# A third pair of k-tiles in the last sweep of w_down, three residues of that sweep by accumulating DMA

## The chip, the cores and the metric

One core of one Trainium2 chip runs the kernel. The metric is device time in microseconds (us) of one execution. TensorE is called PE here, VectorE DVE, ScalarE ACT, GpSimd POOL and SyncE SP, as in the profile; a name with a trailing "q" is that engine's sequencer.

## The reference

The kernel computes one layer of a residual block for 256 tokens of width 2048, in float32. The part in front (differential attention beside a convolution, and their output projection) is not touched. The change is in the last matrix product of the second half:

```python
hn = rms_norm(h, norm2_g[l])
a = jnp.einsum('bsd,df->bsf', hn, w_gate[l].astype(hn.dtype))      # 2048 -> 5632
bu = jnp.einsum('bsd,df->bsf', hn, w_up[l].astype(hn.dtype))       # 2048 -> 5632
h = h + jnp.einsum('bsf,fd->bsd', jax.nn.silu(a) * bu, w_down[l].astype(hn.dtype))
```

## The kernel before, in words

**Precision.** PE reads float32r. Every operand is split into a rounded part `hi` and a residue `lo`, and each product is three matmuls: hi by hi, lo by hi, hi by lo. For a tile of weights, `raw` is loaded by SP (L320), ACT rounds it into `whi` (L325) and DVE subtracts to get `wlo` (L334). There is a second way to the residue, used where `by_dma` is set: ACT writes the negative of the rounded weights into `wlo` (L328), and POOL issues a DMA (L329) that adds `raw` into it, from SBUF to SBUF; DVE then has nothing to do for that tile.

**The hidden width in groups.** The 5632 hidden columns are 11 blocks of 512, that is 4 k-tiles of 128 each, taken in groups of 4, 4 and 3 blocks (`FGROUPS`). After the gate and up products of a group's blocks follows a pass of `w_down` over the k-tiles of that group (`down_pass`). A pass has two sweeps: the first makes the output columns 0 to 1023, the second 1024 to 2047. In a sweep the left 512 columns are called g and the right 512 u. The last group (g = 2) has 12 k-tiles.

**Pairs and twos.** In a sweep some k-tiles are taken as pairs: tile p with tile p + 4, against both column halves at once. The 2 x 2 blocks of a pair are multiplied with seven products in place of eight (`PRODUCTS`, L1046 to L1048: 7 x 3 = 21 matmuls), for which sums of the four weight blocks are formed: on DVE L1019, L1020 and L1021 write the sums `wt`; ACT rounds the blocks (L1022) and the sums (L1025); DVE makes the residues `wlb` (L1028) and `wlt` (L1029). A pair's first four products use the sums, so its third matmul is the first that reads `wlt`. The other k-tiles go as "twos": two k-tiles against one column half, 12 matmuls (L1067, L1068, and L1073 for the last four, which read `wlo`). The sums of the activations that a pair needs are made once for a group (`make_down_forms`, L903 to L944), from `raw_act`, to which the transposed activations are copied (`transposed`); `NDS` gives the number of pairs for which these forms are made.

**The order of units.** `DORDERS` writes out the order in a sweep: s is a pair, g and u are twos. I number the units of the last group's sweeps: A0 to A9 for the first ("gguusggsuu", pairs A4 and A7), B0 to B9 for the second ("gggsgsuuuu", pairs B3 and B5). The program runs one unit after another (`run_chunks`). Before the matmuls of unit t are issued, units up to t + 2 are split (residues on DVE; for a pair also ACT's L1025) and units up to t + 3 are loaded and rounded (for a pair also DVE's sums and ACT's L1022; for a two by DMA also ACT's L328 and POOL's L329), where a pair is among t to t + 3; elsewhere it is t + 2 for both. Each engine works its instructions in that order, so the order of these steps is the order on DVE, ACT and POOL. Buffers: five `raw`, three `whi`, three `wlo`, two `wb` (a pair's weights), one `wt`. A load is issued when the unit that had its buffer has been split, or, for a unit by DMA, when that unit's turn has come.

**The end of a sweep.** Once the last unit that isn't a u is done, ACT copies one bank (L1156) and DVE adds the seven products up (L1158 to L1163, `bank_sums`); after the last u the other half follows. For the first sweep of the last group POOL then adds the four results into `hd` in DRAM (L1210 twice, L1238 twice, behind DVE's L1226), SP fetches the other half of `hd` (`hend`, L1200), and some units later POOL copies the finished half of `hd` to the output (L1245, twice), which waits for these four. For the second sweep DVE adds into `hend` (L1212, L1217, L1278, L1231), and that goes to the output. All DMAs issued by POOL are on one queue (q0), all by SP on another (q1).

Of the kernel before, what the change touches and what calls it, by code (L numbers as in the profile page):

```python
# [84 lines left out]
ORDER = "sggsggsuusuu"  # L85
# [1 line left out]


HD = N // P
NDS = (4, 4, 2)  # L90
DORDERS = {4: (ORDER, ORDER), 3: ("gguusggsuu", "gggsgsuuuu")}
HD_LAG = 3
DOWN_BY_DMA = {4: (dict(g=(0, 1), u=(1,)),) * 2, 3: (dict(g=(), u=()),) * 2}

Q1, Q6, Q7, Q5, Q2, Q4, Q3, QX = range(8)

# [31 lines left out]
def tile_block(  # L128
# [6 lines left out]
    act, dve, pool, pe, sp = nc.scalar, nc.vector, nc.gpsimd, nc.tensor, nc.sync  # L135
# [96 lines left out]
    def lhs_two(pfx, k):  # L232
        return tuple(lhs.tile([P, 2, S], F32R, tag=f"l{x}", name=f"{pfx}{x}{k}") for x in ("hi", "lo"))
# [12 lines left out]
    def start(gen):  # L246
        running.append(gen)
# [7 lines left out]
    def lag(n):  # L255
        for _ in range(n):
            yield
# [593 lines left out]
    def up_done(j, ps):  # L851
        fp = ffn["pool"]
        aa = []
        for m in range(NM):
            a = fp.tile([P, N], F32, tag=f"sum{2 + m}", name="a")
            dve.scalar_tensor_tensor(a, ps[m], rstd2[m], sil[m], ALU.mult, ALU.mult)
            aa.append(a)
        yield from lag(4)
        yield from transposed(j, aa)

    def transposed(j, aa):
        last = j + 1 in FIRSTS and NDS[group_of(j)[0]] < HD
        b = j - group_of(j)[1]
        for t in range(N // P // 2):

            pool_, tag = (acc_ps, "acc") if last else (aux_ps, "aux")
            pt = pool_.tile([P, 2, S], F32, tag=tag, name="ps_a")
            for i in range(2):
                for m in range(NM):
                    c = (2 * t + i) * P  # L870
                    pe.transpose(pt[:, i, m * P : (m + 1) * P], aa[m][:, c : c + P], ident)  # L871
            g = group_of(j)[0]
            nd = NDS[g]
            if b < 2 and 2 * t < nd:
                if not b and not t:
                    raw_act[g] = ffn["pool"].tile([P, 2, nd, S], F32, tag="draw", name="raw_act")
                act.copy(raw_act[g][:, b, 2 * t : 2 * t + 2, :], pt)
                yield from lag(3 if last else 6)
                if b and 2 * t + 2 == nd:
                    start(make_down_forms(g))  # L880
                continue
            hi, lo = lhs_two("a", j * (N // P) + 2 * t)
            act.copy(hi, pt)
            yield from lag(1 if last else 2)
            dve.tensor_tensor(lo, pt, hi.bitcast(F32), ALU.subtract)
            for i in range(2):
                actT[j * (N // P) + 2 * t + i] = (hi[:, i, :], lo[:, i, :])
            yield from lag(1 if last else 3 if closing(j) else 4)

    def closing(j):  # L890
        return j + 1 in FIRSTS and NDS[group_of(j)[0]] == HD

    def group_of(j):

        j0 = 0
        for g, nb in enumerate(FGROUPS):
            if j < j0 + nb:
                return g, j0
            j0 += nb

    raw_act = {}
    down_forms = {}

    def make_down_forms(g):

        nd = NDS[g]
        gap = lambda: lag(5 if FGROUPS[g] == 4 else 2)
# [195 lines left out]
    def fast_block(order, pairs, twos, sources, operands, half, whole, by_dma=dict(g=(), u=())):  # L1103

        units, sums = [], {}
        left = dict(s=list(pairs), g=list(twos), u=list(twos))
        for kind in order:
            what = left[kind].pop(0)
            c = dict(kind=kind, sums=sums, done=None, first={}, last={}, rows=what["rows"], **operands)
            if kind == "s":  # L1110
                c.update(p=what["p"], fetch=load_pair, by_dma=False, round=round_pair, split=split_pair, multiply=multiply_pair,
                         uses=[q for q, _, _ in PRODUCTS])
                c["from"] = sources
            else:
                w, col = sources[kind]
                c.update(ks=what["ks"], w=w, nk=2, width=N, cols=[(col, N)], by_dma=what["k"] in by_dma[kind],
                         load=load_chunk, round=round_chunk, split=split_chunk, multiply=multiply_two,
                         uses=(Q3, QX) if kind == "u" else (Q2, Q4))
            units.append(c)
        assert not any(left.values())  # L1120
        for q in range(8):
            users = [c for c in units if q in c["uses"]]
            users[0]["first"][q] = users[-1]["last"][q] = True
        [c for c in units if c["kind"] != "u"][-1]["done"] = half
        units[-1].update(done=whole, prompt=True)
        chunks.extend(units)
# [8 lines left out]

    def down_pass(g, j0, nb):
        k0 = j0 * HD
        nd = NDS[g]
        ks = [k for k in range(nb * HD) if k >= 2 * HD or k % HD >= nd]
        twos = [dict(ks=(k0 + a, k0 + b), rows=slice(k0 + a, k0 + b + 1, b - a), k=i)  # L1140
                for i, (a, b) in enumerate(zip(ks[::2], ks[1::2]))]
        for i, order in enumerate(DORDERS[nb]):
            n = 2 * i
            end = {}
            fast_block(order, [dict(p=p, rows=slice(k0 + p, k0 + p + HD + 1, HD)) for p in range(nd)], twos,
                       dict(g=(w_down, n * N), u=(w_down, (n + 1) * N)),
                       dict(pairs=lambda: down_forms.get(g), plain=actT.get),
                       lambda sums, n=n, end=end: down_half(g, n, sums, end),
                       lambda sums, n=n, end=end: down_whole(g, n, sums, end), DOWN_BY_DMA[nb][i])

# [23 lines left out]
    def block_done(j, q):  # L1174
        while "u" not in halfway:
            yield
        u = halfway.pop("u")
        for m, i in enumerate((Q3, QX)):
            dve.tensor_tensor(u[m], q[i], u[m], ALU.add)
        while "g" not in halfway:  # L1180
            yield
        g = halfway.pop("g")
        for m in range(NM):
            dve.tensor_tensor(u[m], u[m], g[m], ALU.mult)
        yield from lag(6 if closing(j) else 4)
        yield from transposed(j, u)
# [15 lines left out]
    def down_half(g, n, q, end):  # L1202
        gs, us = yield from bank_sums(q)
        if not at_end(g, n):
            end.update(us=us)
            yield from lag(HD_LAG)
        for m in range(NM):
            cs = slice(n * N, (n + 1) * N)
            if not at_end(g, n):
                pool.dma_start(out=hd[m][:, cs], in_=gs[m], accum_op=ALU.add)  # L1210
            else:
                dve.tensor_tensor(hend[m][:, :N], hend[m][:, :N], gs[m], ALU.add)  # L1212
                pool.dma_start(out=out[m * P : (m + 1) * P, cs], in_=hend[m][:, :N])
        yield
        if at_end(g, n):
            for m in range(NM):
                dve.tensor_tensor(hend[m][:, N:], hend[m][:, N:], us[m], ALU.add)  # L1217
        end.update(us=us)

    def down_whole(g, n, q, end):  # L1220
        while "us" not in end:
            yield
        us = end["us"]
        for m, i in enumerate((Q3, QX)):
            if not at_end(g, n):
                dve.tensor_tensor(us[m], q[i], us[m], ALU.add)  # L1226
                continue
            w = N // 2
            for a in range(0, N, w):
                hs = hend[m][:, N + a : N + a + w]  # L1230
                dve.tensor_tensor(hs, hs, q["ends"][a // w] if m else q[i][:, a : a + w], ALU.add)  # L1231
                (act if m and a else sp).dma_start(
                    out=out[m * P : (m + 1) * P, (n + 1) * N + a : (n + 1) * N + a + w], in_=hs)
        if not at_end(g, n):
            if FGROUPS[g] > 3:
                yield from lag(HD_LAG)
            for m in range(NM):
                pool.dma_start(out=hd[m][:, (n + 1) * N : (n + 2) * N], in_=us[m], accum_op=ALU.add)  # L1238
        if g == len(FGROUPS) - 1 and not at_end(g, n):
            fetch_end()  # L1240

            yield from lag(6)
            for m in range(NM):
                cs = slice(n * N, (n + 2) * N)
                pool.dma_start(out=out[m * P : (m + 1) * P, cs], in_=hd[m][:, cs])  # L1245
# [87 lines left out]
```

## Time and profile before

| | |
|---|---|
| median of three runs | 1036.0 us (1035.3 to 1036.17) |
| the profiled execution | 1035.99 us |
| its span, first to last instruction | 1034.2 us |
| mean granted PE clock | 1.000 |
| busy: PE, DVE, ACT, POOL | 1028.1, 927.3, 638.3, 108.7 us |
| PE, 998.4 to 1019.5 us of the span | 20.87 of 21.10 us busy |
| DVE, the same stretch | 20.10 us busy |
| ACT, the same stretch | 11.28 us busy |

The last pass of `w_down` begins at about 966 us; its first sweep ends at 998.4, its second at about 1030. Rows of a timeline give the start in us of the span, the duration in us, the engine, the line, the operation with output and input, the shapes and how many instructions were merged; brackets give the idle time just ahead and what ended it. A row with "x3" covers three instructions back to back. Durations on PE overlap, as matmuls are pipelined; the distance between starts is the pace.

### The profile page before, as it was taken

The numbers are of one execution on the slowest core, as the hardware profiler recorded it, in microseconds if no ns is written. First come the engines' busy times: TensorE is split into PE (matmuls) and PEld (weight loads), VectorE is DVE, ScalarE is ACT, GpSimd is POOL, SyncE is SP. The second block draws the span as 40 slices with busy tenths as digits, with TensorE's granted clock in tenths as the row PEclk, the third lists the DMA queues.
The fourth block names the chain that finished last, engine by engine and source line by source line (L and its number), as shares of the span: only waits on it lengthen the run. The fifth ranks groups of instructions, "written<-read, shape, count | busy, mean of one in ns | idle before, by whom it ended". The sixth has DMA issues, their size and how long they took to land.

```text
span 1034.2 us, 13010 instructions
## 1 busy us (share of the span) xinstructions
PE 1028.1 (99%) x4645; PEld 848.9 (82%) x4645; DVE 927.3 (90%) x1126; ACT 638.3 (62%) x780; POOL 108.7 (11%) x147
## 2 busy tenths in 40 slices
PE   9999999999999999999999999999999999999998
PEld 7888888888888888888888888888888888888886
DVE  7899999989766699999999898989999989989887
ACT  7554656655666575677666556667657556667452
POOL 0130112111000100100102111001001111000010
PEclk9999999999999999999999999999999999999999
DMA  9657654553546677987989899879798979797773
GB/s 340 225 182 276 215 175 145 183 183 135 183 171 223 189 258 226 286 256 211 260 260 257 265 255 271 267 225 261 230 270 248 280 214 298 231 262 230 218 219 106
DMA packets 115664, 237.59 MB, mean 230 GB/s; under 512 B 7696, under 2 KB 8848, under 8 KB 115344
## 3 DMA queue, kind: packets, MB, share of 16 engines
q1 hardware_dynamic: 104720, 203.58, 59.0%
q0 software_dynamic: 10592, 33.04, 16.5%
q8 instruction: 36, 0.59, 0.2%
q14 instruction: 28, 0.23, 0.1%
q10 hardware_dynamic: 288, 0.16, 0.1%
HBM read 204.24 MB, written 9.44 MB: 207 GB/s over the span
## 4 chain that ended last, share of the span: by engine, by line
PE 96%; DVE 2%; DMA 1%; issue 1%; ACT 0%; SPq 0%; DVEq 0%
PE acc L364 11%; PE acc L365 11%; PE acc L370 11%; PE q L1067 11%; PE q L1068 11%; PE q L1073 11%; PE q L1048 9%; PE q L1046 9%; PE q L1047 9%; PE ps_a L871 1%; DVE wlo L334 1%; DMA raw<-in_w_in_dram 1%; PE ps_s L692 1%; PE ps_o L762 1%; DVE wlt L1029 0%
## 5 line engine op out<-in xcount | busy, mean ns | idle before, releaser
L325 ACT CAST whi<-raw 128x1024 fp32r<-128x1024 f32 (+1 forms) x257 | 266.4, 1047 | 149.7 <-PE acc L365 87.5
L334 DVE TENSOR_TENSOR wlo<-raw,whi 128x1024 fp32r<-128x1024 f32 (+1 forms) x211 | 254.6, 1217 | 37.9 <-ACT whi L325 37.8
L1025 ACT CAST wh<-wt 128x2048 fp32r<-128x2048 f32 x60 | 114.9, 1915 | 108.8 <-DVE wt L1021 108.7
L1029 DVE TENSOR_TENSOR wlt<-wt,wh 128x2048 fp32r<-128x2048 f32 x60 | 137.4, 2290 | 19.5 <-ACT wh L1025 19.4
L364 PE MATMUL acc<-whi,xhi 128*128 128x512 f32 x320 | 127.2, 398 | 0.7 <-ACT whi L325 0.6
L1067 PE MATMUL q<-whi,chi 128*128 128x512 f32 x320 | 125.2, 391 | 0.0
L365 PE MATMUL acc<-whi,xlo 128*128 128x512 f32 x320 | 125.1, 391 | 0.0
L1068 PE MATMUL q<-whi,clo 128*128 128x512 f32 x320 | 124.6, 389 | 0.0
L1046 PE MATMUL q<-wh,fhi 128*128 128x512 f32 x280 | 109.9, 392 | 0.0
L1047 PE MATMUL q<-wh,flo 128*128 128x512 f32 x280 | 108.9, 389 | 0.0
L1028 DVE TENSOR_TENSOR wlb<-wb,wh 128x1536 fp32r<-128x1536 f32 x60 | 105.1, 1751 | 1.1 <-ACT wh L1022 1.1
L553 DVE SCALAR_TENSOR_TENSOR y<-upad,cw,y 128x256 f32<-128x256 f32 x240 | 102.2, 485 | 2.2 <-ACT y L546 2.2
L329 POOL DMA_DIRECT2D wlo<-raw x46 | 39.8, 865 | 508.0 <-ACT wlo L328 283.4
L1022 ACT CAST wh<-wb 128x1536 fp32r<-128x1536 f32 x60 | 88.3, 1472 | 0.0
L370 PE MATMUL acc<-wlo,xhi 128*128 128x512 f32 x320 | 87.1, 393 | 0.0
L1073 PE MATMUL q<-wlo,chi 128*128 128x512 f32 x320 | 85.6, 389 | 0.0
L1067 PE MATMUL q<-whi,ahi 128*128 128x512 f32 x190 | 74.1, 390 | 0.0
L1068 PE MATMUL q<-whi,alo 128*128 128x512 f32 x190 | 74.0, 389 | 0.0
L1019 DVE TENSOR_TENSOR wt<-wb 128x1024 f32<-128x1024 f32 x60 | 73.1, 1218 | 0.0
L364 PEld LDWEIGHTS acc<-whi,xhi 128*128 128x128 f32 x320 | 60.3, 189 | 14.5 <-ACT whi L325 2.0
L365 PEld LDWEIGHTS acc<-whi,xlo 128*128 128x128 f32 x320 | 60.3, 188 | 12.3
L1073 PEld LDWEIGHTS q<-wlo,chi 128*128 128x128 f32 x320 | 60.1, 188 | 12.6
(253 smaller groups left out, 1836.3 us busy)
## 6 DMA issues: line engine op xcount, KB each, us to landing
raw<-in_w_in_dram SPq DMA_DIRECT2D x79, 512.0 KB, 4.7
raw<-in_w_gate_dram SPq DMA_DIRECT2D x48, 512.0 KB, 5.3
raw<-in_w_up_dram SPq DMA_DIRECT2D x48, 512.0 KB, 5.3
raw<-in_w_down_dram SPq DMA_DIRECT2D x48, 512.0 KB, 6.4
wlo<-raw POOLq DMA_DIRECT2D x46, 512.0 KB, 7.1
wb<-in_w_up_dram SPq DMA_DIRECT2D x40, 512.0 KB, 4.5
wb<-in_w_gate_dram SPq DMA_DIRECT2D x40, 512.0 KB, 5.8
wb<-in_w_down_dram SPq DMA_DIRECT2D x40, 512.0 KB, 6.0
```

The costliest lines, as they stand in the source:

```text
L325: act.copy(c["hi"], c["raw"])
L334: dve.tensor_tensor(c["lo"], c["raw"], c["hi"].bitcast(F32), ALU.subtract)
L364: pe.matmul(ps[m], xhi[:, ms], hi[:, j, :], start=c["first"] and j == 0, stop=False)
L365: pe.matmul(ps[m], xlo[:, ms], hi[:, j, :], start=False, stop=False)
L370: pe.matmul(ps[m], xhi[:, ms], lo[:, j, :], start=False, stop=c["last"] and j == nk - 1)
L1025: act.copy(c["hi"][:, :SUMMED], c["t"])
L1029: dve.tensor_tensor(lot, c["t"], c["hi"][:, :SUMMED].bitcast(F32), ALU.subtract)
L1046: pe.matmul(ps, hi, c["hi"][:, w], start=bool(first), stop=False)
L1047: pe.matmul(ps, lo, c["hi"][:, w], start=False, stop=False)
L1067: pe.matmul(ps, xs[i][0][:, ms], hi[:, i, :], start=i == 0 and bool(c["first"].get(qs[m])), stop=False)
L1068: pe.matmul(ps, xs[i][1][:, ms], hi[:, i, :], start=False, stop=False)
L1073: pe.matmul(sum_bank(c, qs[m]), xs[i][0][:, ms], lo[:, i, :], start=False, stop=i == 1 and bool(c["last"].get(qs[m])))
```

## The change

The second sweep of the last group takes three pairs (k-tiles 0 to 2 of the group with 4 to 6) and six twos, in the order "gsgsgsuuu": pairs B1, B3 and B5, and units B0 to B8. The first sweep keeps two pairs. The forms of that group are made for three pairs, and the k-tiles 2 and 6, which are twos in the first sweep and a pair in the second, are kept in both shapes. In the second sweep the residues of the first two g twos (B0, B2) and of the first u two (B6) go by accumulating DMA; before, none in these two sweeps did.

```diff
-NDS = (4, 4, 2)
-DORDERS = {4: (ORDER, ORDER), 3: ("gguusggsuu", "gggsgsuuuu")}
+NDS = (4, 4, 3)
+PASS_PAIRS = ((4, 4), (4, 4), (2, 3))
+DORDERS = {4: (ORDER, ORDER), 3: ("gguusggsuu", "gsgsgsuuu")}
 HD_LAG = 3
-DOWN_BY_DMA = {4: (dict(g=(0, 1), u=(1,)),) * 2, 3: (dict(g=(), u=()),) * 2}
+DOWN_BY_DMA = {4: (dict(g=(0, 1), u=(1,)),) * 2, 3: (dict(g=(), u=()), dict(g=(0, 1), u=(0,)))}
...
                     raw_act[g] = ffn["pool"].tile([P, 2, nd, S], F32, tag="draw", name="raw_act")
-                act.copy(raw_act[g][:, b, 2 * t : 2 * t + 2, :], pt)
-                yield from lag(3 if last else 6)
-                if b and 2 * t + 2 == nd:
+                end = min(2 * t + 2, nd)
+                act.copy(raw_act[g][:, b, 2 * t : end, :], pt[:, : end - 2 * t])
+                if 2 * t + 2 <= PASS_PAIRS[g][0]:
+                    yield from lag(3 if last else 6)
+                if b and end == nd:
                     start(make_down_forms(g))
-                continue
+                if 2 * t + 2 <= PASS_PAIRS[g][0]:
+                    continue
...
     def down_pass(g, j0, nb):
         k0 = j0 * HD
-        nd = NDS[g]
-        ks = [k for k in range(nb * HD) if k >= 2 * HD or k % HD >= nd]
-        twos = [dict(ks=(k0 + a, k0 + b), rows=slice(k0 + a, k0 + b + 1, b - a), k=i)
-                for i, (a, b) in enumerate(zip(ks[::2], ks[1::2]))]
         for i, order in enumerate(DORDERS[nb]):
+            nd = PASS_PAIRS[g][i]
+            ks = [k for k in range(nb * HD) if k >= 2 * HD or k % HD >= nd]
+            twos = [dict(ks=(k0 + a, k0 + b), rows=slice(k0 + a, k0 + b + 1, b - a), k=i)
+                    for i, (a, b) in enumerate(zip(ks[::2], ks[1::2]))]
             n = 2 * i
```

## The prediction

> **What bounds the kernel now.** I read the page first, for the bound and the time outside the span; then the timelines of PE, DVE, ACT, POOL and SP over the last 80 us, because the edit acts there; then the DMA view of the same stretch.
>
> ```profile
> span 1034.2 us, 13010 instructions
> PE 1028.1 (99%) x4645; PEld 848.9 (82%) x4645; DVE 927.3 (90%) x1126; ACT 638.3 (62%) x780; POOL 108.7 (11%) x147
> PE 96%; DVE 2%; DMA 1%; issue 1%; ACT 0%; SPq 0%; DVEq 0%
> ```
>
> PE is the bound: it is busy for 99% of the span and is 96% of the chain that ended last. The profiled execution took 1035.99 us: 1034.2 of span and 1.8 around it. It sits on the median of the runs (1036.0), so a change of the span is added to 1036.0 directly. A difference under about 0.2% (2.07 us) can't be told from no change.
>
> The units of the sweep that changes, in the naming above, stand on PE like this. The rows of L1067 and L1046 are first matmuls: of B0, B1, B3, B4, B5, B6 and the last unit, B9. The two of L1048 are the third matmuls of the pairs B3 and B5:
>
> ```profile
> 998.36 0.39 PE L1067 MATMUL q<-whi,ahi 128*128 128x512 f32 x1
> 1001.08 0.39 PE L1067 MATMUL q<-whi,ahi 128*128 128x512 f32 x1
> 1006.52 0.39 PE L1046 MATMUL q<-wh,dhs 128*128 128x512 f32 x1
> 1007.03 0.50 PE L1048 MATMUL q<-wlt,dhs 128*128 128x512 f32 x1
> 1011.47 0.39 PE L1067 MATMUL q<-whi,ahi 128*128 128x512 f32 x1
> 1014.19 0.39 PE L1046 MATMUL q<-wh,dhs 128*128 128x512 f32 x1
> 1015.03 0.50 PE L1048 MATMUL q<-wlt,dhs 128*128 128x512 f32 x1 [0.23 <-DVE wlt L1029]
> 1019.47 0.39 PE L1067 MATMUL q<-whi,ahi 128*128 128x512 f32 x1
> 1027.63 0.39 PE L1067 MATMUL q<-whi,ahi 128*128 128x512 f32 x1
> ```
>
> B0, twelve matmuls, takes 1001.08 - 998.36 = 2.72 us, so a matmul costs 0.2267 us and a pair of 21 should take 4.76. The two pairs took 1011.47 - 1006.52 = 4.95 and 1019.47 - 1014.19 = 5.28: stalls of 0.19 and 0.52, 0.71 together, both at the third matmul, the first that reads the residue `wlt`. So here PE is the bound with DVE right behind it.
>
> **What goes from PE.** The second sweep had 2 pairs and 8 twos, 2 x 21 + 8 x 12 = 138 matmuls; now 3 pairs and 6 twos, 135. Three matmuls less are 0.68 us. That is the whole arithmetic saving; the rest is decided by whether the operands come in time.
>
> **DVE, walked in the new order.** Its rows of before give duration and pitch:
>
> ```profile
> 987.32 3.49 DVE L334 TENSOR_TENSOR wlo<-raw,whi 128x1024 fp32r<-128x1024 f32 x3
> 992.38 0.69 DVE L1158 TENSOR_TENSOR sum<-q,sum 128x512 f32<-128x512 f32 x1 [1.57 <-ACT sum L1156]
> 996.37 1.22 DVE L334 TENSOR_TENSOR wlo<-raw,whi 128x1024 fp32r<-128x1024 f32 x1
> 998.11 1.29 DVE L1226 TENSOR_TENSOR sum<-q,sum 128x512 f32<-128x512 f32 x2 [0.52 <-PE q L1073]
> 999.31 1.21 DVE L1019 TENSOR_TENSOR wt<-wb 128x1024 f32<-128x1024 f32 x1
> 1001.28 0.69 DVE L1021 TENSOR_TENSOR wt<-wt,wb 128x512 f32<-128x512 f32 x1
> 1001.89 1.22 DVE L334 TENSOR_TENSOR wlo<-raw,whi 128x1024 fp32r<-128x1024 f32 x1
> 1003.03 1.75 DVE L1028 TENSOR_TENSOR wlb<-wb,wh 128x1536 fp32r<-128x1536 f32 x1
> 1004.70 2.28 DVE L1029 TENSOR_TENSOR wlt<-wt,wh 128x2048 fp32r<-128x2048 f32 x1
> 1006.90 1.22 DVE L334 TENSOR_TENSOR wlo<-raw,whi 128x1024 fp32r<-128x1024 f32 x1
> 1010.01 0.69 DVE L1021 TENSOR_TENSOR wt<-wt,wb 128x512 f32<-128x512 f32 x1
> 1012.69 2.29 DVE L1029 TENSOR_TENSOR wlt<-wt,wh 128x2048 fp32r<-128x2048 f32 x1 [0.31 <-ACT wh L1025]
> ```
>
> By start to start a two's residue occupies DVE for 1.14 us, L1019 to L1021 of a pair 2.58 (999.31 to 1001.89), L1028 1.67 and L1029 2.20: 6.45 for a pair. The sweep costs DVE 2 x 6.45 + 8 x 1.14 = 22.0 us before. After, three of six twos' residues go to the DMA: 3 x 6.45 + 3 x 1.14 = 22.8. So DVE gets 0.8 us more in total; what matters is the order, since the first pair is now due at 1001.08 and not at 1006.52.
>
> The first pair's sums fall into the idle 1.57 us ahead of L1158. Of the three residues from 987.32 the third (B0's) is gone, so L1019 of B1 can start at 989.6 and the three end at 992.2, just before 992.38. The six sums keep their place (992.38 to 996.4), as ACT's copy sets their start. Then L1028 and L1029 of B1 run 996.4 to 1000.3; PE wants `wlt` at 1001.08 + 0.45 = 1001.53: met by 1.2 us. L1226 moves to 1000.3 (nobody on PE needs that bank before 1005.2), then B3: L1019 1001.4, L1028 1004.0, L1029 1006.1 (2.68 after the start of L1021, as from 1010.01 to 1012.69) to 1008.4, wanted at 998.36 + 45 x 0.2267 + 0.45 = 1009.01: met by 0.6. B4's residue 1008.3, B5: L1019 1009.5, L1021 1011.4, L1029 1014.1 to 1016.4, wanted at 1016.04 + 0.45 = 1016.49: met by under 0.1. So both old stalls go (0.71 us), the last with no margin at all; I take it at zero, with up to 0.5 us as its bad end, what the same place lost before.
>
> With every operand in time the last unit would thus start 0.68 + 0.71 = 1.39 us earlier, at 1026.24. DVE has this to do beside the last units, now three and not four:
>
> ```profile
> 1018.93 0.69 DVE L1158 TENSOR_TENSOR sum<-q,sum 128x512 f32<-128x512 f32 x1 [0.55 <-ACT sum L1156]
> 1025.23 1.29 DVE L1217 TENSOR_TENSOR hend<-hend,sum 128x512 f32<-128x512 f32 x2
> ```
>
> L1158 came 4.74 us after B5's first matmul, 4.22 without the stall, and L1217 was done 7.6 us later, 6.5 without the one residue in between. So after: 1020.3 to 1026.8, while the last unit's first bank, six matmuls after 1026.24, is ready at 1027.6. The cover of three units is enough, by 0.8 us; whatever it lacked would come on top.
>
> **The forms.** Eleven DVE operations of 256 elements become 384 wide, 0.13 us more each (0.42 against 0.69 us for 512), 1.5 us in the block ahead; ACT gets seven such and two copies. The first row ends the forms, the second follows 2.23 us of idle time that ACT and PE set:
>
> ```profile
> 957.47 0.42 DVE L941 TENSOR_TENSOR dls<-dsums,dls 128x256 fp32r<-128x256 f32 x1
> 960.13 0.69 DVE L1158 TENSOR_TENSOR sum<-q,sum 128x512 f32<-128x512 f32 x1 [2.23 <-ACT sum L1156]
> ```
>
> So the 1.5 us is taken from idle time and costs nothing; were that cover gone, at most 1.5 us.
>
> **The three residues by DMA.** Each adds an ACT pass of 1.05 us, an issue on POOL and a transfer on the POOL queue. Rows of the transfers (the fourth is of the accumulating line over the whole span, issue to landing), and what stands on POOL's queue:
>
> ```profile
> 996.35 1.78 POOL L1210 DMA_DIRECT2D hd<-sum x2 [40.59 <-DVE sum L1162]
> 999.15 1.76 POOL L1238 DMA_DIRECT2D hd<-sum x2 [1.02 <-DVE sum L1226]
> 1008.55 0.59 POOL L1245 DMA_DIRECT2D out_dram<-hd x1 [7.63 <-DMA hd<-sum]
> 1011.03 0.54 POOL L1245 DMA_DIRECT2D out_dram<-hd x1 [1.90 <-DMA hd<-sum]
> DMA to landing us min/median/max: 5.4/7.1/9.6
> DMA to landing us min/median/max: 5.3/5.4/5.5
> ```
>
> (The last is of L1245.) ACT's rows:
>
> ```profile
> 987.50 1.05 ACT L325 CAST whi<-raw 128x1024 fp32r<-128x1024 f32 x1 [0.52 <-ACT whi L325]
> 1010.74 1.92 ACT L1025 CAST wh<-wt 128x2048 fp32r<-128x2048 f32 x1 [4.49 <-DVE wt L1021]
> 1012.56 2.94 ACT L325 CAST whi<-raw 128x1024 fp32r<-128x1024 f32 x3
> ```
>
> B0: the rounded copy is the first row, the negative follows to 989.6, so the residue, 5.4 to 9.6 us after its issue, lands between 995.0 and 999.2; wanted at 998.36 + 8 x 0.2267 = 1000.17: hidden. B2: its buffers come free with A8, which ends 2.72 us (A9) ahead of B0, at 995.6; ACT is done at 997.0, landing 1002.4 to 1006.6, wanted at 1005.84 + 8 x 0.2267 = 1007.65: hidden. But two things stand behind it on POOL: the L1210 pair moves from 996.35 to about 998.2, and all later transfers of this queue line up behind the residue. That they finish one after another is seen in L1245: its two starts are 2.5 us apart though the two L1238 that release them were issued within 1.8.
>
> B6 is the one that decides. ACT can only make its negative after L1025 of B5, which follows DVE's L1021 (about 1012.1): L1025 to 1014.1, the rounded copy to 1015.0, the negative to 1016.0. But on POOL the two L1245 come first, and they wait for the four sums in DRAM. How late those get, by the DMA view of 997 to 1010.5 (two rows) and of 946.5 to 950.5 (one accumulate of 512 KB, the third row):
>
> ```profile
> q0 software_dynamic: 599, 1.14, 53.2%
> q1 hardware_dynamic: 796, 2.03, 42.9%
> q0 software_dynamic: 137, 0.51, 70.3%
> ```
>
> Of 13.5 us the POOL queue used 7.2, of which some 0.5 (an estimate: 1010 to 1010.5) belong to the first L1245: 6.7 us for four sums. SP's queue used 5.8 for 2 MB. The accumulate used 0.703 x 4 = 2.8. After, from B2's first packets (about 999.4): 2.8 + 6.7 on POOL's queue, and on SP's 2.5 MB (B5's 1 MB of weights, which wait for L1028 of B1 at 998.1 with `hend` and B8's load queued behind, then those), 7.3 us. All of it would be through at 999.4 + 16.8 = 1016.2; if a third of SP's 7.3 us comes behind the sums, these are through at 1013.8. An issue follows a landing by some tenths. I take 1016.1 for the second L1245, in place of 1011.03: near the end with both queues shared out, as they were before. It lands 5.5 later, at 1021.6, and B6's residue follows with its 2.8 us: 1024.4. PE wants it at 1020.80 + 8 x 0.2267 = 1022.62: a stall of 1.8 us. Bounds: 0 (L1245 by 1014.3) and 3.9 (1016.9 + 9.6 = 1026.5).
>
> **Sum.** -0.68 - 0.71 + 1.8 = +0.4: span 1034.6, time 1036.4, which a measurement can't tell from no change.
>
> [...]
>
> **The rivals.** *No stall at B6*: L1245 starts by 1014.3, the residue is issued at 1016.1 and lands in the least time seen, 5.4 us, at 1021.5. For it: SP's queue has little left after 1014. Against: 5.4 is the least of 46, and POOL's queue isn't empty. Time 1036.0 - 1.4 = 1034.6. [...] Chance 0.25.
>
> *Slower: B6's residue sets the end.* The same place, but three transfers in line ahead of it stretch as L1238's did: PE waits at B6's ninth matmul for longer than the change saves. It decides from a landing of 1022.62 + 1.39 = 1024.0 on, and by over 0.2% from 1026.1. With the second L1245 at 1017.0 and the longest landing, 9.6, the residue is there at 1026.6: a stall of 4.0, +2.6, time 1038.6. For it: POOL's queue gets 2.8 us more work and starts its sums later. Against: SP's traffic should be over by then. Chance of over 0.2%: 0.16.
>
> *B5's weights come late.* The third pair's 1 MB is asked for at 998.1 and needed at 1009.5; at SP's 43% share its 2.9 us of work take some 7. If it comes 2 us late, PE stalls about 2 us at B5, B6's residue is then hidden, sum +0.6, time 1036.6. Chance 0.07.
>
> **The numbers.** The forecast (a stall of 0.4 to 3.4 at B6, 1035.0 to 1038.0) has 0.52. Faster by over 0.2% would need 2.07 us where 1.39 is the most to be had: 0.02, cut from the first rival, for a wait that I overlook. Slower by over 0.2%: the second rival's 0.16 and 0.02 of the third, 0.18. Within: 0.80. The range takes in the no-stall case and the forecast's upper end with its unknowns: 1034.5 to 1038.2.
>
> **What would show it.** L1048 without a wait at B1, B3 and B5; second-sweep L1029 ends near 1000.3, 1008.4, 1016.4; L1245 at about 1013.5 and 1016; B6's L329 right behind it; the first L1073 of B6 delayed past 1022.6 with a DMA named; last unit starting near 1028.0. Wrong if PE waits at a pair, if B6's residue is there by 1022.6, or if PE loses time ahead of 998.

## The result, and the profile after

The changed kernel takes 1039.62 us (median of six runs, 1037.55 to 1040.96) beside 1036.09 for the kernel before in the same sessions: a ratio of 1.0033 with a 95% interval of 1.0023 to 1.0043. The forecast was 1036.4 within 1034.5 to 1038.2. The kernel is slower by 3.5 us, outside the range, in the place that the second rival named: a wait at B6's ninth matmul. The profiled execution took 1039.49 us, with a span of 1037.7.

Behind `transposed` line numbers are four higher in the changed kernel and nearly all experiments (five in the last one with zero matmuls): L1048 is L1052, L1073 is L1077, L1029 is L1033, L1245 is L1249; the accumulating DMA L329 is L330.

The page of the changed kernel, span, PE and the chain:

```profile
span 1037.7 us, 13020 instructions
PE 1028.3 (99%) x4642; PEld 849.3 (82%) x4642; DVE 929.7 (90%) x1126; ACT 643.5 (62%) x785; POOL 111.4 (11%) x150
PE 94%; DMA 3%; DVE 2%; issue 1%; ACT 0%; SPq 0%; POOL 0%; DVEq 0%; POOLq 0%
```

Three matmuls fewer and yet 3.5 us more span; in the chain 3% are now DMA, where before it was 1%. The waits of PE over the whole program, longest first, name it (columns: total us, times, longest):

```profile
PE q L1077 <- DMA wlo<-raw: 2.8, 1, 2.8
PE ps_warm L163 <- POOL neghalf L157: 1.4, 1, 1.4
PE acc L365 <- ACT whi L326: 1.2, 1, 1.2
```

PE's timeline, first matmuls of B0, B1, B3, B5 and B6, the end of B6's first half, its second half, B7's first matmuls and the last unit:

```profile
998.40 0.39 PE L1071 MATMUL q<-whi,ahi 128*128 128x512 f32 x1
1001.12 0.39 PE L1050 MATMUL q<-wh,dhs 128*128 128x512 f32 x1
1008.60 0.39 PE L1050 MATMUL q<-wh,dhs 128*128 128x512 f32 x1
1016.08 0.39 PE L1050 MATMUL q<-wh,dhs 128*128 128x512 f32 x1
1020.94 0.39 PE L1071 MATMUL q<-whi,ahi 128*128 128x512 f32 x1
1022.52 0.39 PE L1072 MATMUL q<-whi,alo 128*128 128x512 f32 x1
1025.74 1.89 PE L1077 MATMUL q<-wlo,ahi 128*128 128x512 f32 x4 [2.83 <-DMA wlo<-raw]
1027.43 0.63 PE L1071 MATMUL q<-whi,ahi 128*128 128x512 f32 x1
1027.86 0.63 PE L1072 MATMUL q<-whi,alo 128*128 128x512 f32 x1
1031.10 0.39 PE L1071 MATMUL q<-whi,ahi 128*128 128x512 f32 x1
```

Up to B6 it is as forecast: 22.54 us from B0 to B6, 99 matmuls at 0.2267 and 0.1 over. B6's second half was due at 1020.94 + 8 x 0.2267 = 1022.75 and began at 1025.74: 2.99 us of wait. Then comes what no line of the prediction has: the matmuls of B7 start 0.43 us apart and not 0.227. The windows show why (each row ends with the granted clock, the DMA share and GB/s):

```profile
1016.00:1022.60 6.60, 6.60 (x31) 5.22 (x29) 4.88 (x7) 2.56 (x3) 1.51 (x3) 1.00 0.74 163
1022.70:1025.70 3.00, 0.21 (x1) 0.00 (x0) 3.00 (x6) 0.00 (x0) 0.30 (x1) 1.00 0.82 163
1025.70:1029.30 3.60, 3.56 (x9) 2.78 (x10) 1.15 (x2) 0.00 (x0) 0.82 (x2) 0.54 0.40 146
1029.30:1034.00 4.70, 4.70 (x27) 3.98 (x25) 1.82 (x4) 0.00 (x0) 0.00 (x0) 0.99 0.01 2
```

For 3.6 us after the wait PE's granted clock was 0.54 on the mean (0.50 in the windows 1027 to 1028 and 1028 to 1029). From B6's second half to the last unit 16 matmuls took 1031.10 - 1025.74 = 5.36 us where 3.63 are their pace: 1.73 us lost. The sum of the last unit's start, 1031.10 against 1027.63: 0.04 (B0 later) - 0.68 - 0.71 + 0.10 + 2.99 + 1.73 = +3.47 us, and the span grew by 3.5.

Why the residue was late, on POOL's timeline:

```profile
997.38 0.88 POOL L330 DMA_DIRECT2D wlo<-raw  x1 [6.49 <-ACT wlo L329]
997.93 2.13 POOL L1214 DMA_DIRECT2D hd<-sum  x2
1001.32 1.75 POOL L1242 DMA_DIRECT2D hd<-sum  x2 [1.26 <-DVE sum L1230]
1015.48 0.58 POOL L1249 DMA_DIRECT2D out_dram<-hd  x1 [12.41 <-DMA hd<-sum]
1017.66 0.54 POOL L1249 DMA_DIRECT2D out_dram<-hd  x1 [1.59 <-DMA hd<-sum]
1018.35 0.90 POOL L330 DMA_DIRECT2D wlo<-raw  x1
DMA to landing us min/median/max: 7.4/7.4/7.4
```

(The last row is the landing of that last L330.) The two copies to the output waited 12.41 and 1.59 us for the four sums, and B6's residue, ready since 1016.0, could only be issued behind them. It landed at 1025.7.

### The profile page after: what moved, and what is told of

It is laid out like the page before. It is cut to its first block, busy times and chain, and to the rows that moved or that the text cites. A ratio compares the mean times of both kernels' runs of the same rounds, so it can differ in the third digit from the quotient of the medians.

```text
span 1037.7 us, 13020 instructions
## 1 busy us (share of the span) xinstructions
PE 1028.3 (99%) x4642; PEld 849.3 (82%) x4642; DVE 929.7 (90%) x1126; ACT 643.5 (62%) x785; POOL 111.4 (11%) x150
## 4 chain that ended last, share of the span: by engine, by line
PE 94%; DMA 3%; DVE 2%; issue 1%; ACT 0%; SPq 0%; POOL 0%; DVEq 0%; POOLq 0%
PE acc L365 11%; PE acc L366 11%; PE acc L371 11%; PE q L1077 11%; PE q L1071 10%; PE q L1072 10%; PE q L1052 9%; PE q L1050 9%; PE q L1051 9%; DMA hd<-sum 1%; PE ps_a L872 1%; DMA wlo<-raw 1%; DMA raw<-in_w_in_dram 1%; PE ps_s L693 1%; PE ps_o L763 0%
## 5 line engine op out<-in xcount | busy, mean ns | idle before, releaser
L335 DVE TENSOR_TENSOR wlo<-raw,whi 128x1024 fp32r<-128x1024 f32 (+1 forms) x206 | 248.9, 1218 | 37.2 <-ACT whi L326 37.2
L1029 ACT CAST wh<-wt 128x2048 fp32r<-128x2048 f32 x61 | 116.8, 1915 | 110.6 <-DVE wt L1025 110.5
L1033 DVE TENSOR_TENSOR wlt<-wt,wh 128x2048 fp32r<-128x2048 f32 x61 | 139.7, 2291 | 19.8 <-ACT wh L1029 19.7
L330 POOL DMA_DIRECT2D wlo<-raw x49 | 42.5, 867 | 548.8 <-ACT wlo L329 289.6
L1077 PE MATMUL q<-wlo,chi 128*128 128x512 f32 x320 | 85.6, 389 | 0.0
L1071 PE MATMUL q<-whi,ahi 128*128 128x512 f32 x182 | 71.6, 394 | 0.0
L1072 PE MATMUL q<-whi,alo 128*128 128x512 f32 x182 | 71.3, 392 | 0.0
L1077 PEld LDWEIGHTS q<-wlo,chi 128*128 128x128 f32 x320 | 60.1, 188 | 12.6
```

Of the source, the lines that this page charges most:

```text
L335: dve.tensor_tensor(c["lo"], c["raw"], c["hi"].bitcast(F32), ALU.subtract)
L1029: act.copy(c["hi"][:, :SUMMED], c["t"])
L1033: dve.tensor_tensor(lot, c["t"], c["hi"][:, :SUMMED].bitcast(F32), ALU.subtract)
L1071: pe.matmul(ps, xs[i][0][:, ms], hi[:, i, :], start=i == 0 and bool(c["first"].get(qs[m])), stop=False)
L1072: pe.matmul(ps, xs[i][1][:, ms], hi[:, i, :], start=False, stop=False)
L1077: pe.matmul(sum_bank(c, qs[m]), xs[i][0][:, ms], lo[:, i, :], start=False, stop=i == 1 and bool(c["last"].get(qs[m])))
```

## The experiments

Two explanations stood against each other. Theory Q: the loss is B6's residue alone, late because of the sums and copies that POOL moves, and then PE's lower clock. Theory T: three pairs crowd the stretch (DVE without margin, B5's weights, SP's traffic), and the residue is only where it shows. Each kernel was timed beside the kernel before on the same chip.

**B6's residue back on DVE.**

```diff
-3: (dict(g=(), u=()), dict(g=(0, 1), u=(0,)))}
+3: (dict(g=(), u=()), dict(g=(0, 1), u=()))}
```

> B6's residue goes back to DVE, the two g residues stay on the DMA, three pairs as changed. Theory Q (the loss is B6's residue alone: 3.1 us of wait because its transfer stands behind the two copies to the output on POOL's queue, and then some 1.8 us because PE runs at half clock after the wait): no wait of PE in the second sweep, DVE does the residue in 1.2 us between the pair B5 and the sums, last unit from 1026.3, span 1032.8, time 1034.6, 1.4 us faster than before. Theory T (three pairs crowd the stretch: the weights of B5, DVE without margin, SP's traffic): DVE has even more to do, so PE waits at B5 or B6 by 1 us or more, time 1036 or over.

Measured: 1035.06 us (before 1036.49), ratio 0.9986 (0.9977 to 0.9994). In the last 130 us PE's matmuls waited for nothing. DVE (timeline) does B6's residue as the first of three between the pair B5 and the sums, without a gap ahead:

```profile
1014.63 2.29 DVE L1033 TENSOR_TENSOR wlt<-wt,wh 128x2048 fp32r<-128x2048 f32 x1 [0.31 <-ACT wh L1029]
1016.84 3.49 DVE L335 TENSOR_TENSOR wlo<-raw,whi 128x1024 fp32r<-128x1024 f32 x3
1020.89 0.69 DVE L1162 TENSOR_TENSOR sum<-q,sum 128x512 f32<-128x512 f32 x1 [0.56 <-ACT sum L1160]
```

So three pairs and the two g residues by DMA are a gain of 1.4 us, the size that was forecast for operands in time, and what theory T says of DVE falls: it had room for the residue that was taken from it.

**The copies to the output behind the residue.**

```diff
             fetch_end()
-            yield from lag(6)
+            yield from lag(9)
```

> As changed, but the two copies of the finished half to the output are issued three steps later, behind B6's residue on POOL's queue. Theory Q: B6's residue is issued at 1016.3 and not 1018.35, with only the four sums ahead of it on the queue, which are through by 1017; it lands about 1020 to 1022.5, PE waits 0 to 0.3 us, the clock stays full, time 1034.6 to 1035. A theory that the accumulate is slow by itself (7.4 us whatever stands ahead): it lands at 1023.7, PE waits 1.1 us, time 1035.7.

Measured: 1035.04, ratio 0.9987 (0.9979 to 0.9996). POOL's timeline, and the landing of this L330:

```profile
1016.73 0.86 POOL L330 DMA_DIRECT2D wlo<-raw  x1 [13.28 <-PE q L1077]
1017.48 1.20 POOL L1249 DMA_DIRECT2D out_dram<-hd  x2
DMA to landing us min/median/max: 5.7/5.7/5.7
```

It was issued 1.6 us sooner and took 5.7 us, not 7.4, so it landed at 1022.4, and PE never waited. So 7.4 us is not the accumulate's own time: with the two copies behind it and not ahead of it, the same 512 KB took 1.7 us less.

**The second u two in place of the first.**

```diff
-3: (dict(g=(), u=()), dict(g=(0, 1), u=(0,)))}
+3: (dict(g=(), u=()), dict(g=(0, 1), u=(1,)))}
```

> As changed, but of the u twos the second (B7) and not the first (B6) takes its residue by DMA; the same number of transfers. Theory Q: it lands when B6's did, about 1025.7, but PE wants it 2.72 us later, at 1025.3: a wait of 0.4 us (0 to 1.5 with the spread of the transfers), too short to lower the clock, time 1035.0. Theory T: the transfers as such cost, so little changes: 1038 or over.

Measured: 1035.72, ratio 0.9990 (0.9981 to 0.9999). PE's timeline, B7's second half:

```profile
1026.32 1.20 PE L1077 MATMUL q<-wlo,ahi 128*128 128x512 f32 x4 [0.83 <-DMA wlo<-raw]
1027.36 0.39 PE L1071 MATMUL q<-whi,ahi 128*128 128x512 f32 x1
```

The same number of transfers, landing at 1026.3, later than in the changed kernel; but wanted 2.7 us later, so PE idled 0.83 us. That costs about 0.7 us beside the two kernels without a wait (1035.72 to 1035.05), and the clock stayed at 1.00 (windows of 1019 to 1031). One unit earlier the late residue costs 4.9 us, by the ratios of the changed kernel and of the first experiment (0.0047 x 1036).

**Work for PE during the wait.** Thirteen matmuls of a zero operand, which add zero to the bank of B6's second row.

```diff
             resume()
+            if c is chunks[-3]:
+                for _ in range(13):
+                    pe.matmul(sum_bank(c, qs[1]), zeros, hi[:, 0, :], start=False, stop=False)
             for m in range(NM):
                 second_half(m)
```

In the first version ACT wrote the zero operand ahead of everything else:

> As changed, with 13 matmuls of a zero operand put between B6's first and second half (3 us of PE work that adds zero to the bank), so that PE doesn't idle while the residue is under way. If the pace of 0.43 us a matmul after the wait comes from the idle time: the clock stays at 1.00, the second half starts at about 1025.7 as before, all later matmuls at 0.227, span 1035.9, time 1037.7, 1.8 us less than as changed. If the slow matmuls have another cause (operands, the DMA's traffic): no gain, 1039.5.

Measured: 1044.08, ratio 1.0069 (1.0056 to 1.0082). B5 started 6.2 us later than in the changed kernel, at 1022.32, so the time was lost well ahead of the sweep, and the median tells nothing of the clock. The trace does, twice. In the opening PE now waits 5.25 us for ACT, and the matmuls behind that wait go at about half pace: two start 0.42 us apart, where 0.227 is the pace, and are given 0.63 us each, as behind the wait at B6 (line numbers here are two higher than in the changed kernel):

```profile
10.49 0.80 PE L367 MATMUL acc<-whi,xhi 128*128 128x512 f32 x1 [5.25 <-ACT whi L328]
11.52 0.63 PE L367 MATMUL acc<-whi,xhi 128*128 128x512 f32 x1
11.94 0.63 PE L368 MATMUL acc<-whi,xlo 128*128 128x512 f32 x1
```

The mean granted clock of that execution is 0.999, above the changed kernel's 0.998, so here the slow pace is the only sign; the changed kernel idles 1.24 us in its opening and goes on at 0.23 us a matmul. (That wait began 10.49 - 5.25 = 5.24 us into the span, so PE had run little ahead of it, and it is no exact copy of the wait at B6.) And behind the filled wait at B6 the 16 matmuls took 1035.73 - 1031.96 = 3.77 us, beside 3.63 at their pace and 5.36 in the changed kernel. With the operand written at the end of the first sweep:

> The same 13 matmuls of a zero operand between B6's halves, with the zero operand made at the end of the first sweep and not at the kernel's start, where it held up the opening by 6 us. If idle PE is what lowers the clock: second half of B6 at about 1025.8, all matmuls after it at 0.227 us, span 1035.9, time 1037.7, 1.8 us below the changed kernel's 1039.6. If not: 1039.6 as before.

Measured: 1038.15, ratio 1.0016 (1.0006 to 1.0025). PE's timeline and the windows:

```profile
1023.08 3.14 PE L1104 MATMUL q<-whi,zeros 128*128 128x512 f32 x13
1026.22 1.19 PE L1078 MATMUL q<-wlo,ahi 128*128 128x512 f32 x4
1029.97 0.39 PE L1072 MATMUL q<-whi,ahi 128*128 128x512 f32 x1
1025.00:1028.00 3.00, 2.99 (x14) 2.16 (x13) 2.18 (x4) 0.00 (x0) 1.12 (x2) 1.00 0.38 131
```

The second half starts no sooner, but the 16 matmuls from it to the last unit take 3.75 us in place of 5.36, at a clock of 1.00. By the ratios the kernel is 0.0017 x 1036 = 1.8 us below the changed one. The clock's part of the loss is the idle time of PE, shown by filling it.

**No residue by DMA.**

```diff
-3: (dict(g=(), u=()), dict(g=(0, 1), u=(0,)))}
+3: (dict(g=(), u=()),) * 2}
```

> Three pairs in the new order, no residue by DMA: DVE does all six twos. By DVE's rows the residue of B2 comes between L1230 and the sums of B3, so the residue of pair B3 is done at 1010.7 and wanted at 1009.0: a wait of 1.7 us, and another 0.6 at B5; -1.39 + 2.3 = +0.9, time 1037 to 1037.4 beside 1036.1 to 1036.5 before. If the wait of 1.7 us lowers the clock as the 3 us did, some 1 us more. If instead the g residues by DMA were of no use, PE doesn't wait and the time is 1034.7.

Measured: 1036.77, ratio 1.0004 (0.9995 to 1.0014). PE's two waits, on the timeline:

```profile
1010.01 0.50 PE L1052 MATMUL q<-wlt,dhs 128*128 128x512 f32 x1 [1.32 <-DVE wlt L1033]
1018.01 0.50 PE L1052 MATMUL q<-wlt,dhs 128*128 128x512 f32 x1 [0.23 <-DVE wlt L1033]
```

The pairs B3 and B5 took 6.38 and 5.32 us where 4.76 is their pace: 2.2 us, as worked out from DVE's rows. 1.32 us of idle PE didn't lower the clock in the profiled execution (1.00 in every window from 998.4 on). The three pairs pay only with the g residues off DVE; without them they are worth nothing.

**The DMA part alone.**

```diff
-PASS_PAIRS = ((4, 4), (4, 4), (2, 3))
+PASS_PAIRS = ((4, 4), (4, 4), (2, 2))
-3: ("gguusggsuu", "gsgsgsuuu")}
+3: ("gguusggsuu", "gggsgsuuuu")}
```

> The DMA part alone: two pairs and the old order gggsgsuuuu in the second sweep, residues of the first two g twos (B0, B1) and of the first u two (B6) by DMA; the forms stay made for three pairs. Theory Q: B6's residue is issued behind the two copies to the output at about 1017 and lands at 1024 to 1025, wanted at 1021.3: a wait of 2.7 to 3.7 us and half clock after it, the old stalls at the pairs stay, time 1039 to 1041.5. Theory T (the third pair is to blame): no such wait, 1035.5 to 1036.5.

Measured: 1037.23 (1036.01 to 1038.31), ratio 1.0005 (0.9995 to 1.0015). The wait is there, with two pairs as with three, but in the profiled execution (1037.76) it is 1.13 us and not 3, and five of the ten executions took under 1037:

```profile
1013.98 0.54 POOL L1249 DMA_DIRECT2D out_dram<-hd  x1 [1.67 <-DMA hd<-sum]
1015.25 0.90 POOL L330 DMA_DIRECT2D wlo<-raw  x1 [0.73 <-ACT wlo L329]
1022.88 1.20 PE L1077 MATMUL q<-wlo,ahi 128*128 128x512 f32 x4 [1.13 <-DMA wlo<-raw]
```

I expected the copies at 1017; they started at 1011.72 and 1013.98, as here DVE doesn't hold up L1230 (L1242 starts at 999.46, without a wait, in place of 1001.32), and B5's megabyte was asked for long before (in the kernel before, which has the same order, at 984.82; in the changed one at 998.23). So the u residue by DMA needs no third pair to be late, but with the third pair PE idles another 1.7 us. That much of theory T is true.

**The forms alone.** Two pairs, old order, no residue by DMA; only `NDS` at (4, 4, 3).

> Only the forms of the last group made for three pairs (wider operations on DVE and ACT in the block ahead, two more copies); sweeps, order and residues as before the change. The prediction's step, 1.5 us taken from DVE's idle time: no change, 1036.1 to 1036.5. If they push the sums or the pairs: up to 1.5 us more.

Measured: 1036.38, ratio 0.9997 (0.9988 to 1.0006). The wider forms cost nothing that can be measured.

**One g residue less on the DMA.**

```diff
-3: (dict(g=(), u=()), dict(g=(0, 1), u=(0,)))}
+3: (dict(g=(), u=()), dict(g=(0,), u=(0,)))}
```

> As changed, but B2's residue goes back to DVE; B0's and B6's stay on the DMA. Theory Q: without B2's 2.8 us of work ahead of them the four sums are through at about 1014 in place of 1017, the copies to the output start by 1012.5 and 1014.7, so POOL is free before B6's negative is ready (1017.2, as DVE is 1.1 us later from B3 on); B6's residue lands 1022.8 to 1024. DVE's extra 1.1 us costs PE 0.6 us at B3 and 0.5 at B5, so B6 wants it at 1023.7: a wait of 0 to 0.5, no clock loss, time 1036.0 to 1036.6 on a chip where before takes 1036.5. If B2's transfer has no part in the lateness: B6's residue at 1025.7 still, a wait of 2 us on top, 1038 or over.

Measured: 1036.19, ratio 0.9998 (0.9988 to 1.0007). POOL's timeline and the landing of B6's residue:

```profile
1014.73 0.54 POOL L1249 DMA_DIRECT2D out_dram<-hd  x1 [1.49 <-issue]
1017.58 0.90 POOL L330 DMA_DIRECT2D wlo<-raw  x1 [2.32 <-ACT wlo L329]
DMA to landing us min/median/max: 5.4/5.4/5.4
```

Without B2's transfer the second copy starts 2.9 us sooner, just the 2.8 us of engine time of one accumulate; then B6's residue lands in the least time seen, although the second copy, issued 2.85 us ahead of it, was still under way (the copies of this run landed 5.4 us after their issue on the median). PE waits for the pairs instead (0.39 and 0.22 us idle).

**The copies issued by SP.**

```diff
-                pool.dma_start(out=out[m * P : (m + 1) * P, cs], in_=hd[m][:, cs])
+                sp.dma_start(out=out[m * P : (m + 1) * P, cs], in_=hd[m][:, cs])
```

> As changed, but SP and not POOL issues the two copies of the finished half to the output, at the same place. Theory Q (POOL waits in order, and the copies are ahead on the same queue): B6's residue is issued at 1016.3 and has only the four sums ahead; the copies run beside it on the other queue. It lands at 1021.5 to 1023, PE waits 0 to 0.4 us, time 1034.7 to 1035.3 on a chip where before takes 1036.5. If it is the DMA engines as such that are full, whichever queue the copies are on: landing at 1025, a wait of over 2 us, 1037.5 or over.

Measured: 1038.23 (1035.76 to 1038.90), ratio 1.0015 (1.0006 to 1.0024). Here my expectation was wrong. The residue was issued at 1016.41, as expected, but took 8.5 us:

```profile
1016.41 0.87 POOL L330 DMA_DIRECT2D wlo<-raw  x1 [13.27 <-PE q L1077]
DMA to landing us min/median/max: 8.5/8.5/8.5
1024.96 1.20 PE L1077 MATMUL q<-wlo,ahi 128*128 128x512 f32 x4 [1.99 <-DMA wlo<-raw]
```

So POOL's order is not the whole cause: the residue was late whether the copies stood ahead of it on its queue (7.4 us) or ran beside it on the other (8.5). They cost it little or nothing behind it (5.7 us), or when the last of them was issued 2.85 us ahead (5.4).

Its ten executions also point to the clock's step, though only one of them has a trace. Five have a mean granted clock of 1.000 and took 1035.76 to 1037.82 us; five have 0.998 and took 1038.64 to 1038.90. Between the two groups lies a gap and nothing in it.

## Why the prediction was wrong, point by point

**What bounds the kernel, and the arithmetic saving: right.** PE paces the sweep at 0.227 us a matmul; the last group lost three.

**DVE in the new order: right to under 0.1 us.** The residues of the three pairs were forecast to end at 1000.3, 1008.4 and 1016.4. DVE's timeline:

```profile
998.07 2.29 DVE L1033 TENSOR_TENSOR wlt<-wt,wh 128x2048 fp32r<-128x2048 f32 x1
1006.12 2.29 DVE L1033 TENSOR_TENSOR wlt<-wt,wh 128x2048 fp32r<-128x2048 f32 x1 [0.31 <-ACT wh L1029]
1014.11 2.29 DVE L1033 TENSOR_TENSOR wlt<-wt,wh 128x2048 fp32r<-128x2048 f32 x1 [0.31 <-ACT wh L1029]
```

The old stalls of 0.71 us went, but for 0.1 at B5, where the margin was under 0.1. The kernel without B6's residue on the DMA shows the 1.4 us that this step promised.

**The forms: right**, by the run that has them alone. **The tail: right**: DVE was done with its sums and adds early, and the end follows PE.

**B6's residue: right in kind, too small in size; the wait was put at 1.8 us and was 2.99.** The term that failed is the time at which the four sums are through and the second copy starts. The sums were given 1016.2 as their latest and took until 1016.96; the copy was put at 1016.1 and started at 1017.66. In the DMA view of 997 to 1017 us of the changed kernel the two queues used:

```profile
q0 software_dynamic: 733, 1.61, 47.4%
q1 hardware_dynamic: 1112, 2.64, 40.3%
```

Of 20 us that is 9.5 for POOL's queue, the very 2.8 + 6.7 of the prediction, and 8.1 for SP's, against 7.3. Of POOL's part 0.8 us was done before 999.4; the 16.7 us that were left took the 17.6 us from there to 1017 (the same view from 999.4 on). So nothing of SP's work came behind the sums, where I had hoped for some and chosen a time ahead of the bound; SP's share was 0.8 us short; the engines weren't full all the time (16.7 of 17.6 us); and the second copy started another 0.7 us behind the landing that released it (1016.96 to 1017.66). From the copy on it is as worked out: 1017.66 + 5.5 + 2.8 = 1026.0 forecast by that rule, 1025.7 measured. The second rival had the second copy at 1017.0 and a landing at 1026.6: the nearer of the two. (In the prediction's rows of transfers the accumulating line's landings, 5.4/7.1/9.6, are the fifth row and not the fourth.)

**B5's weights, the third rival: in time.** ACT's last wait for them ended at 1008.0, and DVE, which was to need them at 1009.5, started its sums for B5 at 1009.47 without a wait:

```profile
1008.03 1.48 ACT L1026 CAST wh<-wb 128x1536 fp32r<-128x1536 f32 x1 [0.99 <-DMA wb<-in_w_down_dram]
```

**The clock: missing.** Every case priced a wait by its length. This wait of nearly 3 us cost 1.73 more. Without that, the profiled execution would have taken 1037.8, inside the range: both terms together, the wait 1.2 us too short and the clock at nothing, carried the time out of it. The rows of before could not show it: the longest stall of PE in this stretch cost 0.52 us, and behind it the matmuls went on at 0.23 us. In the changed kernel 2.83 us of idle PE was followed by 3.6 us at a granted clock of 0.54, 0.50 at its lowest. With the 1.73 us on top of its stall of 4.0 us the second rival would have stood at 1040.3 and not at 1038.6 (an estimate from these two numbers).

**The landing of an accumulate, taken from the rows: right.** The rows of before gave 5.4 us as the least of 46; B6's residue took 5.4 at the least in these runs, and 7.4 in the changed kernel.

Two of the edits of this change work against each other: the g residues make the third pair pay, and one of them, by 2.9 us of queue, makes the u residue late. Two kernels of the study are each about 1.4 us faster than before, by the u residue on DVE and by the copies to the output behind it; a third, with B7's residue by DMA in place of B6's, about 1 us.

What stays open: how much idle time lowers the clock. 1.99 us did not and 2.83 did, each in one profiled execution; no run was made between. Executions without a trace suggest that one length does not decide it, though their waits aren't known. One of the six of the changed kernel had a mean clock of 0.999, above the others' 0.997 and 0.998, and took 1037.55, about the time without the clock's term. One of the ten without any residue by DMA had 0.998 and took 1038.44, where the profiled one, with 1.32 us of idle time, took 1036.28. And with the copies issued by SP one took 1037.82 at 1.000, 0.86 us longer than the profiled one with its 1.99 us; if only the wait differed, it was 2.85 us (an estimate) and didn't lower the clock.

## What to carry to other kernels

The residue that decided here was late by what the DMA engines had to move ahead of it: 16.7 us of work on the two queues from 999.4 on took 17.6, and only then was the way free for the copy in front of it. Add up that work from the first packet to the deadline, and take the sum as the time, not as the bound. A wait that idled PE for 2.83 us cost its length and, by the lower clock that followed it (0.54 for 3.6 us), 1.73 us more; one of 1.99 us had no such part. So price a wait of nearly three us twice, the second time as a case of its own with a chance. Put such a transfer where its consumer is one unit later (0.83 us of idle PE in place of 2.83), or put uncritical copies behind it (none). An engine's slack is worth a look before its work is moved away: DVE had room for the residue that cost 4.9 us on the DMA.

## What the runs showed of the hardware

After 2.83 us of idle PE the granted clock was 0.54 for 3.6 us. After 5.25 us, in an opening, two matmuls started 0.42 us apart, where 0.227 is the pace, though the mean granted clock of that execution reads 0.999. After 0.83, 1.13, 1.32 and 1.99 us the clock stayed at 1.00 and the pace, but for the first four matmuls, at 0.23 us, each in one profiled execution. An accumulating DMA of 512 KB within SBUF took 5.4 us from issue to landing with the second copy to the output issued 2.85 us ahead of it, 5.7 with both copies behind it, 7.4 to 8.1 in five kernels with the second copy 0.7 to 1.3 us ahead, and 8.5 with the copies beside it on the other queue.
